# A two-layer hybrid decoder trunk: where the second half of a per-layer input product stands in the order of work

## The chip, the cores and the metric

The kernel runs on one core of one Trainium2 chip. The metric is the device time of one execution in microseconds (us); less is better. Everything is one program: two layers, one after the other, with all weights read from HBM once.

## The reference, cut to what matters

Each of the two layers takes the residual stream h (512 tokens, 1024 features) through three steps:

```
h = h + W_out [ sparse attention heads || mLSTM heads ](RMSNorm(h) @ W_in)
h = h + relu(RMSNorm(h) @ W1)^2 @ W2               # the MLP, 1024 -> 4096 -> 1024
h = h + sigmoid(RMSNorm(h) @ Wg + bg) * (p[i] @ Wp)  # the gated per-layer input, p is 512 x 256
```

The change touches the second and the third step only. p[i] @ Wp, the per-layer input product, does not depend on h at all, so it can be computed at any time before the gate needs it.

## The kernel before, in words

Everything is kept transposed: features on the 128 partitions, the 512 tokens along the free axis. h lies in SBUF as eight tiles of 128x512 (`const` in the trace). Products in float32 are made of three matmuls on a split of each operand into a rounded part hi and a remainder lo: hi*hi, hi*lo, lo*hi (`mm3`).

**Weights.** A weight tile of 128x1024 (512 KB) is loaded by SP into one of 3 buffers `raw`. ScalarE (ACT) writes hi, a rounded copy, into one of 4 buffers `hi`; lo goes into one of 4 buffers `lo`. There are two ways to make lo (`weight`, L521). Most tiles are `adder` tiles: ACT writes -raw rounded, and a DMA issued by GpSimd (POOL) adds. The others subtract hi from raw on VectorE (DVE), or, where `pool` is set, on DVE or POOL as the planner finds it better.

**The MLP** (`mlp`, L1204). Four blocks of the first product (`ff1`) come first. Then 7 shares follow. In share c, two calls of `pair` make four further blocks of the first product, by a scheme with seven products of 12 matmuls with 256 columns each (A12*B21, A11*B11, S1*T1, S2*T2, S3*T3, S4*B22, A22*T4). `pair` gives way (yields) four times, and after each time one output block of the second product of share c (`ff2`) is put in: 12 matmuls with 512 columns, then a DVE add into h. Two output blocks share one weight tile. An eighth share of eight output blocks has no `pair` beside it. The products T1 to T4 use sums of h's tiles, the `forms`, which DVE and ACT make at the MLP's start beside the normal operands (`prep`).

**The per-layer input** (`inputs`, L1180) has two halves, i = 0 and i = 1. Each loads p's two tiles (`s<-pt`, 256 KB each) and one weight tile W_PLE, makes their hi and lo (the label `pw`), and then runs 24 matmuls with 512 columns into four PSUM banks, which ACT copies out (the label `filler`). Half 0 is put into the program ahead of the MLP, half 1 inside the last share, behind its first output block: the buffers and loads of half 1 wait (`nc.hold`) for that block's last operation.

**The gate** (`ple`, L1277) needs the new h, normalised by token, and the four blocks of each half.

**The order.** A planner (`Plan.schedule`, L248) simulates the engines and writes one fixed order for each of the five queues. An operation's rank is the longest way from it to the end, by the planner's own costs, plus 1000 times its label's entry in `URGENT`, and less 1e7 for each later stage; the stages are mix, MLP and gate of layer 0, then of layer 1. A matmul with the label `filler` (-990) is taken only where no other matmul of that stage is ready. `pw` has +145, so these operations go ahead of the MLP's own. Matmuls that carry `nc.chain` keep their program order among themselves: the MLP and the gate are one such chain, `"mlp"`. The filler matmuls are outside it. The planner assumes that a DMA on SP lands 2.2 us after its transfer time, and a DMA from POOL 5.5 us after its issue. At run time each engine works through its queue strictly in this order, and waits on the first instruction that isn't ready. All instructions are issued from one line (L390), so the trace's rows are told apart by tile names and shapes.

Of the kernel before, what the change touches and what calls it, by code (L numbers as in the profile page):

```python
# [33 lines left out]
NFF = 8  # L34
# [9 lines left out]
W_CQ, W_UP, W_QK, W_V, W_O, W_OUT, W_FF1, W_FF2, W_PLE, W_GATE, NW = 0, 2, 4, 12, 16, 20, 28, 60, 92, 94, 102  # L44
# [3 lines left out]

STEP, AHEAD = 5, 8

URGENT = {"start": 325, "squares": 285, "squares0": 90, "setup": -135, "prep": 120, "forms": 120, "norm": 180, "cq": 80, "keys": 55,
          "index": 30, "queries": 45, "gates": 75, "values": 30, "conv": -25, "pw": 145, "filler": -990,
          "attention": -20, "mlstm": 20, "out0": -115, "out1": -145}

# [72 lines left out]
class Plan:  # L127
# [120 lines left out]
    def schedule(self):  # L248
# [9 lines left out]
        for op in ops:  # L258
            op.rank += 1000.0 * (URGENT.get(op.label, 0) + op.bias) - 1e7 * op.stage
        free = {k: list(range(n)) for k, n in self.rooms.items()}  # L260
# [141 lines left out]
class Trunk:  # L402
# [777 lines left out]
    def inputs(self, l, i):  # L1180

        nc = self.nc
        nc.label = "pw"
        raws = [self.slot([128, S]) for _ in range(2)]
        for k in range(2):
            nc.sync.dma_start(raws[k], self.ap["pt"][l, k])
        w = self.wtile(l, W_PLE + i, pool=True)
        pts = []
        for k in range(2):
            hi, lo = self.slot([128, S], F32R), self.slot([128, S], F32R)  # L1190
            nc.scalar.activation(hi, raws[k], AF.Copy)
            nc.vector.tensor_tensor(lo, raws[k], hi.bitcast(F32), op=ALU.subtract)
            pts.append((hi, lo))
        nc.label = "filler"
        for n in range(4):
            ps = self.psum("proj")
            for k in range(2):
                c = slice(k * 512 + n * 128, k * 512 + n * 128 + 128)
                self.mm3(ps, (w[0][:, c], w[1][:, c]), pts[k], k == 0, k == 1)
            o = self.slot([128, S])  # L1200
            nc.scalar.activation(o, ps, AF.Copy, scale=0.5)
            self.pw.setdefault(l, []).append(o)

    def mlp(self, l):  # L1204
        nc = self.nc
        nc.stage = 3 * l + 1
        nc.label = "mlp"
        forms = []
        xs, acc = self.prep(l, C_MLP, forms)
        H = S // 2  # L1210
        lower, upper = slice(0, H), slice(H, S)
        nc.hold = nc.ops[self.mark]
        self.inputs(l, 0)
        nc.hold, nc.label = None, "mlp"
        nc.chain = "mlp"
        fs, state = {}, {}

        def square(i, v):
            hi, lo = self.slot([128, S], F32R), self.slot([128, S], F32R)
            nc.scalar.activation(hi, v, AF.Square)  # L1220
            nc.scalar.activation(v, v, AF.Square)
            nc.vector.tensor_tensor(lo, v, hi.bitcast(F32), op=ALU.subtract)
            fs[i] = (hi, lo)

        def relu(out, u, c=slice(0, S)):
            nc.vector.scalar_tensor_tensor(out, u, 0.0, state["r"][:, c], op0=ALU.max, op1=ALU.mult)

        def ff1(i, n=1, between=None):
            return self.blocks([self.wtile(l, W_FF1 + i + j, adder=True) for j in range(n)], xs, between=between)

        def root():
            state["t"] = self.token_r(acc, D)

        def take(i):
            def act(u0, u1, x):
                relu(u0, u0)
                relu(u1[:, lower], x[:, 0:H], lower)
                relu(u1[:, upper], u1[:, upper], upper)
                square(i, u0)
                square(i + 1, u1)  # L1240
            return act

        def ff2(c):

            for n in range(KD):
                if n % 2 == 0:
                    w = self.wtile(l, W_FF2 + 4 * c + n // 2, adder=True)
                ps = self.psum("proj")
                for k in range(4):
                    o = slice((n % 2) * 512 + k * 128, (n % 2) * 512 + k * 128 + 128)  # L1250
                    self.mm3(ps, (w[0][:, o], w[1][:, o]), fs[4 * c + k], k == 0, k == 3)
                nc.vector.tensor_tensor(self.h[n], self.h[n], ps, op=ALU.add)
                yield n


        pss = ff1(0, 2, root)
        pss += ff1(2)
        state["r"] = self.spread(state["t"])
        pss += ff1(3)
        for i, ps in enumerate(pss):  # L1260
            v = self.slot([128, S], tag="s.v")
            relu(v, ps)
            square(i, v)
        ops = self.operands(xs, forms)
        for c in range(NFF - 1):
            parts = ff2(c)
            for i in (4 * c + 4, 4 * c + 6):
                for _ in self.pair(l, W_FF1 + i, ops, take(i)):
                    next(parts)
        for n in ff2(NFF - 1):  # L1270
            if n == 0:
                nc.hold, nc.chain = nc.ops[-1], None
                self.inputs(l, 1)
                nc.hold, nc.chain, nc.label = None, "mlp", "mlp"
        nc.chain = None

    def ple(self, l):  # L1277
# [138 lines left out]
```

## Time and profile before

| | us |
|---|---|
| median of 3 runs | 1361.09 (1359.71 to 1362.44) |
| the profiled execution | 1356.89 |
| its span (first to last instruction) | 1355.2 |
| TensorE (PE) busy in the span | 1312.2 (97%) |
| VectorE (DVE) busy | 933.1 (69%) |
| ScalarE (ACT) busy | 789.1 (58%) |
| granted TensorE clock, mean | 0.993 |

The trace is of the profiled execution alone. Its 1356.89 us are its span and 1.7 us around it; the median of the separate runs is 4.20 us, or 0.31%, above it. A busy share of PE counts modelled ends of pipelined matmuls, so gaps and the pitch between matmuls say more than the share.

### The profile page before, as it was taken

The page shows a single profiled execution, that of the slowest core. Times are in us where ns is not written, and L with a number is a line of the kernel's source. Part 1 is how long each engine was busy: PE and PEld are TensorE (multiplying, and loading weights), DVE is VectorE, ACT ScalarE, POOL GpSimd, SP SyncE. Part 2 cuts the span into 40 slices and gives each one's busy share as a digit, 9 for nine tenths or more (in the row PEclk, how much of TensorE's full clock was granted, in tenths as well). Part 3 has the DMA queues.
Part 4 walks back from the last instruction along what each step waited for, and adds up shares of the span by engine and source line. Part 5 has one row for each costly group of instructions (what it writes and reads, how often), then busy time and mean ns, then how long its engine had stood idle before and what let it go on. Part 6 is the DMA issues. An engine that isn't in the chain of part 4 may idle for free. (4 is left out here: it accounts for less than half of the span.)

```text
span 1355.2 us, 20154 instructions
## 1 busy us (share of the span) xinstructions
PE 1312.2 (97%) x7376; PEld 1125.9 (83%) x7376; DVE 933.1 (69%) x2049; ACT 789.1 (58%) x1477; POOL 204.5 (15%) x240
## 2 busy tenths in 40 slices
PE   7999999999999999998999999999999999999988
PEld 6877898878888998986887778987798989988877
DVE  7899896576565666644859998848656566665535
ACT  4986684674544545545548947837554554545632
POOL 4132100320100100013112211004010000000210
PEclk9999999999999999999999999999999999999989
DMA  5546801655656555575235576125655655545741
GB/s 191 134 116 170 194 25 44 159 140 156 155 144 161 141 146 140 142 197 144 78 104 125 131 170 166 30 63 140 173 151 145 156 141 156 140 137 140 191 125 63
DMA packets 53092, 183.73 MB, mean 136 GB/s; under 512 B 6272, under 2 KB 6784, under 8 KB 52992
## 3 DMA queue, kind: packets, MB, share of 16 engines
q1 hardware_dynamic: 34848, 116.37, 26.5%
q0 software_dynamic: 18144, 66.07, 26.2%
q8 instruction: 58, 0.95, 0.3%
q14 instruction: 42, 0.34, 0.1%
HBM read 114.25 MB, written 2.10 MB: 86 GB/s over the span
## 5 line engine op out<-in xcount | busy, mean ns | idle before, releaser
L390 PE MATMUL ps_proj<-s,hi 128*128 128x512 f32 (+1 forms) x3184 | 848.7, 356 | 8.0 <-DVE s L390 6.8
L390 PEld LDWEIGHTS ps_proj<-s,hi 128*128 128x128 f32 x3184 | 558.7, 189 | 99.4 <-DVE s L390 9.9
L390 PE MATMUL ps_proj<-s,lo 128*128 128x512 f32 (+1 forms) x1592 | 561.2, 355 | 11.5 <-DVE lo L390 11.5
L390 ACT ACTIVATE hi<-raw 128x1024 fp32r<-128x1024 f32 (+1 forms) x212 | 221.9, 1049 | 253.1 <-PE ps_proj L390 170.9
L390 PEld LDWEIGHTS ps_proj<-s,lo 128*128 128x128 f32 x1592 | 300.3, 189 | 57.1 <-DVE lo L390 13.2
L390 POOL DMA_DIRECT2D lo<-raw x126 | 108.9, 864 | 932.1 <-ACT lo L390 839.7
L390 DVE TENSOR_TENSOR const<-const,ps_proj 128x512 f32<-128x512 f32 x160 | 109.4, 686 | 162.9 <-PE ps_proj L390 162.7
L390 DVE TENSOR_TENSOR lo<-raw,hi 128x1024 fp32r<-128x1024 f32 (+1 forms) x86 | 105.3, 1225 | 115.6 <-ACT hi L390 67.9
L390 ACT ACTIVATE lo<-raw 128x1024 fp32r<-128x1024 f32 x126 | 132.4, 1051 | 9.6 <-PE ps_proj L390 6.5
L390 PE MATMUL ps_proj<-hi,s 128*128 128x512 f32 (+1 forms) x384 | 113.4, 382 | 8.3 <-ACT hi L390 7.6
L390 ACT ACTIVATE s<-s 128x512 fp32r<-128x512 f32 (+2 forms) x154 | 89.3, 619 | 28.9 <-DVE s L390 16.5
L390 DVE TENSOR_TENSOR s<-s,s 128x512 fp32r<-128x512 f32 (+2 forms) x124 | 86.9, 732 | 16.2 <-ACT s L390 15.5
L390 PEld LDWEIGHTS ps_proj<-hi,s 128*128 128x128 f32 x384 | 70.6, 195 | 18.6 <-ACT hi L390 7.6
L390 PE MATMUL ps_sc<-s,s 128*128 128x512 f32 (+3 forms) x288 | 83.4, 376 | 0.6 <-ACT s_idx L390 0.2
L390 POOL TENSOR_TENSOR s<-s,s 128x512 f32<-128x512 f32 x42 | 62.9, 1498 | 91.5 <-ACT s L390 80.8
L390 ACT ACTIVATE s<-ps_proj 128x256 f32<-128x256 f32 (+1 forms) x104 | 41.9, 415 | 54.1 <-PE ps_proj L390 54.1
L390 PE MATMUL ps_proj<-lo,s 128*128 128x512 f32 (+1 forms) x192 | 65.9, 382 | 1.3 <-DVE lo L390 1.3
L390 ACT ACTIVATE s<-raw 128x512 fp32r<-128x512 f32 x28 | 17.6, 628 | 85.0 <-DVE raw L390 85.0
L390 PEld LDWEIGHTS ps_sc<-s,s 128*128 128x128 f32 x288 | 50.6, 190 | 10.6 <-issue 2.2
L390 DVE MATCH_REPLACE8 s<-m,s 128x384 f32<-128x384 f32 (+2 forms) x96 | 51.3, 539 | 0.0
L390 DVE MAX8 m<-s 128x8 f32<-128x384 f32 (+2 forms) x96 | 48.9, 544 | 0.2 <-POOL s L390 0.2
L390 PE MATMUL ps_po<-at,s_et 128*128 128x64 f32 x320 | 48.7, 255 | 0.0
(149 smaller groups left out, 1566.3 us busy)
## 6 DMA issues: line engine op xcount, KB each, us to landing
raw<-ws SPq DMA_DIRECT2D x204, 512.0 KB, 3.6
lo<-raw POOLq DMA_DIRECT2D x126, 512.0 KB, 5.2
raw<-wa SPq DMA_DIRECT2D x8, 336.0 KB, 3.2
const<-xt SPq DMA_DIRECT2D x8, 256.0 KB, 4.6
s<-pt SPq DMA_DIRECT2D x8, 256.0 KB, 7.5
out<-const SPq DMA_DIRECT2D x7, 256.0 KB, 2.0
const<-ct SPq DMA_DIRECT2D x2, 132.0 KB, 3.1
out<-const SPq DMA_DIRECT2D x2, 128.0 KB, 1.7
```

What stands on the lines that cost most here:

```text
L390: ins = getattr(getattr(nc, e), method)(*[value(x) for x in args], **{k: value(x) for k, x in kw.items()}).ins
```

## The change: what it does

1. `inputs` is cut in two. `inputs` now makes the operands only (loads, hi, lo) and returns them; the new `filler` runs the matmuls and the copies. Half 0 calls one behind the other, as before.
2. For half 1, the operands are put into the program ahead of the eighth share, and wait for the last operation of an earlier point (`ahead`): the second `yield` of the last `pair`, that is, ACT's copy of its S2*T2 product. Before, they waited for the first output block of the eighth share.
3. The matmuls of half 1 come behind all output blocks of the eighth share and in the chain `"mlp"`: fixed between the last matmul of the MLP and the first of the gate.
4. For half 1, lo of W_PLE is made on DVE only (`pool=not i`).
5. In each share, the first `yield` of the first `pair` is passed without an output block, so each block of the second product comes one place later, and the eighth one follows behind the second `pair`.
6. `URGENT["forms"]` goes from 120 to 40; `prep` stays at 120.

```
-URGENT = {..., "prep": 120, "forms": 120, "norm": 180, ...
+URGENT = {..., "prep": 120, "forms": 40, "norm": 180, ...

     def inputs(self, l, i):
...
-        w = self.wtile(l, W_PLE + i, pool=True)
+        w = self.wtile(l, W_PLE + i, pool=not i)
         pts = []
         for k in range(2):
             hi, lo = self.slot([128, S], F32R), self.slot([128, S], F32R)
             nc.scalar.activation(hi, raws[k], AF.Copy)
             nc.vector.tensor_tensor(lo, raws[k], hi.bitcast(F32), op=ALU.subtract)
             pts.append((hi, lo))
+        return w, pts
+
+    def filler(self, l, w, pts):
+        nc = self.nc
         nc.label = "filler"
         for n in range(4):
...
-        self.inputs(l, 0)
+        self.filler(l, *self.inputs(l, 0))
...
         for c in range(NFF - 1):
-            parts = ff2(c)
+            parts, n = ff2(c), 0
             for i in (4 * c + 4, 4 * c + 6):
                 for _ in self.pair(l, W_FF1 + i, ops, take(i)):
-                    next(parts)
-        for n in ff2(NFF - 1):
-            if n == 0:
-                nc.hold, nc.chain = nc.ops[-1], None
-                self.inputs(l, 1)
-                nc.hold, nc.chain, nc.label = None, "mlp", "mlp"
+                    if n == 5:
+                        ahead = nc.ops[-1]
+                    if n:
+                        next(parts)
+                    n += 1
+            next(parts)
+        nc.hold = ahead
+        rest = self.inputs(l, 1)
+        nc.hold, nc.label = None, "mlp"
+        for _ in ff2(NFF - 1):
+            pass
+        self.filler(l, *rest)
         nc.chain = None
```

## Rows read from the trace of the kernel before

**Rows 1.** Stretches: us, busy us (instructions) of PE, PEld, DVE, ACT, POOL; clock, DMA share, GB/s

```profile
574.00:595.00 21.00, 21.00 (x131) 18.71 (x131) 11.31 (x19) 10.86 (x16) 2.58 (x3) 1.00 0.62 152
595.00:617.00 22.00, 22.00 (x97) 17.74 (x96) 8.79 (x13) 12.88 (x20) 5.10 (x6) 1.00 0.76 190
```

**Rows 2.** Timeline of PE, both layers' MLP tails: start, duration, operation, [idle before, releaser]

```profile
627.55 0.80 PE L390 MATMUL ps_proj<-s,lo 128*128 128x512 f32 x1 [4.63 <-DVE lo L390]
...
1293.86 1.22 PE L390 MATMUL ps_proj<-s,lo 128*128 128x512 f32 x2 [3.55 <-DVE lo L390]
```

**Rows 3.** The stretches just behind the two stalls of group 2

```profile
627.50:631.00 3.50, 3.45 (x9) 2.73 (x10) 0.66 (x1) 3.50 (x7) 1.53 (x1) 0.54 0.80 274
...
1293.90:1300.00 6.10, 6.10 (x15) 4.80 (x16) 0.57 (x1) 0.67 (x2) 1.51 (x1) 0.52 0.46 173
```

**Rows 4.** Timeline of DVE in the tail of layer 0

```profile
599.35 0.75 DVE L390 SCALAR_TENSOR_TENSOR s<-const,const,s 128x512 fp32r<-128x512 f32 x1 [0.79 <-ACT s L390]
...
616.51 4.28 DVE L390 SCALAR_TENSOR_TENSOR s<-const,const,s 128x512 fp32r<-128x512 f32 x2 [1.53 <-ACT s L390]
...
625.69 0.67 DVE L390 TENSOR_TENSOR const<-const,ps_proj 128x512 f32<-128x512 f32 x1
626.29 1.21 DVE L390 TENSOR_TENSOR lo<-raw,hi 128x1024 fp32r<-128x1024 f32 x1
```

**Rows 5.** Timeline of ACT, then SP, in the tail of layer 0

```profile
611.15 0.63 ACT L390 ACTIVATE s<-s 128x512 fp32r<-128x512 f32 x1 [7.58 <-DMA s<-pt]
...
603.18 0.91 SPq L390 DMA_DIRECT2D s<-pt  x2
```

**Rows 6.** Timeline of PE, stalls inside the two layers' MLPs

```profile
275.33 0.50 PE L390 MATMUL ps_proj<-s,hi 128*128 128x512 f32 x1 [0.92 <-DVE s L390]
...
277.46 0.50 PE L390 MATMUL ps_proj<-s,hi 128*128 128x512 f32 x1 [1.17 <-DVE s L390]
...
303.24 0.50 PE L390 MATMUL ps_proj<-s,hi 128*128 128x512 f32 x1 [1.02 <-DVE s L390]
...
1219.88 0.39 PE L390 MATMUL ps_proj<-s,lo 128*128 128x256 f32 x1 [0.91 <-DVE lo L390]
1243.21 0.39 PE L390 MATMUL ps_proj<-s,lo 128*128 128x256 f32 x1 [2.00 <-DVE lo L390]
```

**Rows 7.** Timeline of DVE just before the stalls at 275 and 277

```profile
272.48 2.80 DVE L390 TENSOR_TENSOR s<-s,s 128x256 f32<-128x256 f32 x4
...
275.53 0.67 DVE L390 TENSOR_TENSOR const<-const,ps_proj 128x512 f32<-128x512 f32 x1
```

**Rows 8.** First and last pair: PE's last A11*B11 matmul, DVE's add of it

```profile
299.53 0.28 PE L390 MATMUL ps_proj<-vx,lo 128*128 128x256 f32 x1
...
301.97 0.42 DVE L390 TENSOR_TENSOR s<-s,ps_proj 128x256 f32<-128x256 f32 x1 [1.24 <-ACT s L390]
...
1245.79 0.28 PE L390 MATMUL ps_proj<-vx,lo 128*128 128x256 f32 x1
...
1246.87 0.41 DVE L390 TENSOR_TENSOR s<-s,ps_proj 128x256 f32<-128x256 f32 x1
```

**Rows 9.** One adder tile through ACT and POOL, ACT's next wait, PEld's wait

```profile
585.48 1.04 ACT L390 ACTIVATE lo<-raw 128x1024 fp32r<-128x1024 f32 x1
...
591.65 0.63 ACT L390 ACTIVATE s<-s 128x512 fp32r<-128x512 f32 x1 [5.12 <-DVE s L390]
...
586.82 0.86 POOL L390 DMA_DIRECT2D lo<-raw  x1 [5.32 <-ACT lo L390]
...
586.35 0.19 PEld L390 LDWEIGHTS ps_proj<-s,lo 128*128 128x128 f32 x1 [0.18 <-DMA lo<-raw]
```

**Rows 10.** DMA issues: tiles, queue, count, KB each, median us to landing

```profile
raw<-ws SPq DMA_DIRECT2D x204, 512.0 KB, 3.6
lo<-raw POOLq DMA_DIRECT2D x126, 512.0 KB, 5.2
...
s<-pt SPq DMA_DIRECT2D x8, 256.0 KB, 7.5
```

More of the change, by code (lines that the diff above doesn't have):

```diff
@@ L49 @@
 STEP, AHEAD = 5, 8
-URGENT = {"start": 325, "squares": 285, "squares0": 90, "setup": -135, "prep": 120, "forms": 120, "norm": 180, "cq": 80, "keys": 55,
+URGENT = {"start": 325, "squares": 285, "squares0": 90, "setup": -135, "prep": 120, "forms": 40, "norm": 180, "cq": 80, "keys": 55,
           "index": 30, "queries": 45, "gates": 75, "values": 30, "conv": -25, "pw": 145, "filler": -990,
```

## The prediction

> **What bounds the kernel now.** I read the stretches first, then the list of PE's stalls, and for each stall the queue of the engine that ended it. In the steady MLP the matmuls leave no gap: 21 and 22 us busy out of 21 and 22, at a granted clock of 1.00 [rows 1]. From 97 matmuls with 512 columns in 22 us I take 0.23 us for one. There nothing is to be won by moving work between the other engines; only PE's stalls count. The reader should look for two groups of them.
>
> The large ones stand behind the MLP, one in each layer: PE waits 4.63 us and 3.55 us for a lo that DVE makes [rows 2]. Afterwards the clock is at the lower of its two levels for a while: 0.54 of full speed over 3.50 us in layer 0, 0.52 over 6.10 us in layer 1 [rows 3]. That costs (1 - 0.54) x 3.50 = 1.6 us and (1 - 0.52) x 6.10 = 2.9 us more. Why is that lo late? In that place only W_PLE of half 1 is a tile of 128x1024 whose lo DVE makes; the gate's first tiles go through POOL. DVE reaches it at 626.29, straight behind the last add into h at 625.69 [rows 4], though PE had been waiting since 627.55 - 4.63 = 622.92. DVE is behind because two of `prep`'s operations, which take 0.75 us each elsewhere, take 4.28 us together at 616.51 [rows 4], and because the whole tail began late: ACT, with p's hi at the head of its queue, stood still 7.58 us until 611.15, as SP had issued p's loads only at 603.18 [rows 5]. So half 1 is both late itself and holds up the gate's operands.
>
> The small ones are at the MLP's start (0.92, 1.17 and 1.02 us in layer 0, and the same three in layer 1), and 0.91 and 2.00 us late in layer 1 only [rows 6].
>
> **The change part by part.** No work is added or removed: the same loads, copies and matmuls run, and DVE made W_PLE's lo for half 1 before, too. All is a matter of order.
>
> *Half 1's operands ahead.* They now wait for ACT's copy of S2*T2 in the last pair. One block (12 x 0.23 = 2.8 us) is already passed over there, and from that copy to the end of the MLP come 12 more output blocks and three small products, some 37 us. Loads of 7.5 us, two hi, two lo and W_PLE's own hi and lo fit in many times. PE then goes from the last output block into the 24 matmuls without a wait: the stalls of 4.63 + 3.55 us and the 1.6 + 2.9 us of low clock go: -12.7 us. What is late next? The gate's first matmuls. Between the MLP and the gate stand half 0's and half 1's matmuls, up to 48 x 0.23 = 11 us as before, and ACT's 7.58 us of standing still in this place are gone too, so `prep` is earlier. I count nothing against the 12.7; the bounds are in a rival.
>
> *The wait moves to the last pair.* ACT will stand at p's hi there: the planner reckons some 3 us from issue to landing, the trace shows 7.5 us [rows 10], so ACT waits about 4.5 us, and DVE, with p's lo, with it. Behind it in ACT's queue stand the next weight tile and the squares for the last share. Before, ACT had a gap of 5.12 us just there, waiting for DVE until 591.65 [rows 9]. So I take 0; if the cover were gone it would be up to 4.5 us a layer.
>
> *A buffer fewer.* W_PLE of half 1 now holds one of the 4 `hi` and one of the 4 `lo` buffers from the last pair to the end of the MLP, and half 0's W_PLE holds another, because its matmuls run only when nothing else can. Two remain for the last share's four adder tiles. Such a tile takes ACT 2 x 1.04, POOL 0.86 [rows 9] and 5.2 us to land [rows 10], about 8.1 us, and then serves 24 matmuls, 5.5 us. Three buffers turn over every 13.6/3 = 4.5 us, less than 5.5, and the trace shows that this is just in time: one matmul waited 0.18 us for such a lo [rows 9]. Two turn over every 6.8 us. The tile that gets its buffer only when A22*T4 is done is needed two output blocks later (5.5 us), so 2.6 to 2.8 us are missing, and as much again two tiles on: 5.6 us a layer at most. But half 0's 24 matmuls (5.5 us) are there to fill just such gaps, and the planner puts them where it foresees one. Between 0 and 5.6 I take 1.5 a layer, nearer to the filled case: +3.0 us.
>
> *Forms at 40.* The stalls at 275.33 and 277.46 wait for `prep`'s lo on DVE [rows 6], and just before them DVE runs forms (halves of 256 columns, 2.80 us for four) [rows 7]. With `prep` above `forms` these go: up to 0.92 + 1.17 us in layer 0 and the same two in layer 1, 4.2 us. But DVE has the same work to do, and the late adds into h (275.53) hold up `prep` as well. Between 0 and -4.2 I take half: -2.1 us.
>
> *Output blocks one place back.* At the first pair, the block whose matmul waited 1.02 us for the squares (303.24) [rows 6] comes 2.8 us later: this stall goes. But S2*T2 now follows A11*B11 after S1*T1 alone (12 matmuls of half the width, 1.4 us), and it writes the bank that DVE's add must have read. That add ended at 302.39, 2.6 us after A11*B11's last matmul [rows 8], so 1.2 us of waiting appear. 0 in sum, between -2.1 and +2.4 over both layers. In the 26 pairs behind the two first ones the same add never ended later than in the last, at 1247.28, 1.2 us after [rows 8]: no wait. In layer 1 the stall of 0.91 us stands at the first pair of a share, which now begins 2.8 us later: -0.9. The one of 2.00 us stands at a second pair, where nothing shifts: it stays.
>
> *A rule weighed.* The last pair's stretch keeps the DMA engines busy 0.62 of the time at 152 GB/s [rows 1]; the 1.0 MB that moves there would need 0.62/152 x 1.0 MB = 4.3 us of full use, and 0.38 x 21 = 8 us are free. The Trainium skill, "DMA: Bandwidth & Descriptors", section "Issuing engines are not separate DMA queues", says that transfers started from any engine end on the same 16 DMA engines and interleave. By the row the move costs 0; by the rule the 4.3 us would fall on the tiles, a rival below.
>
> **The sum.** -12.7 + 3.0 - 2.1 + 0 - 0.9 = -12.7 us, made against the profiled execution: 1356.89 - 12.7 = 1344.2 us. The median of the runs shown stands 4.20 us above that execution, so I forecast a median of 1361.09 - 12.7 = 1348.4 us. Its own range is 1343 to 1354. A measurement of this kernel can tell about 0.2%, 2.7 us, from no change.
>
> **The rivals.**
> *The ring runs dry (slower).* W_PLE's place in the ring is the mechanism, in the last share's eight blocks. If the planner doesn't put half 0's matmuls into these gaps, or puts them where the chip doesn't have the gap, 5.6 us open in each layer, and a gap of nearly 3 us can bring the low clock back (1.6 us or more). If the adder's landing is 2 us longer in that crowd than its median, each of two gaps grows by 2: 5.6 + 4 + 2 = 11.6 a layer, +23 us against -15.7: 1368. It decides from about 8 us a layer. For it speaks the wait of 0.18 us; against it the 24 matmuls that may fill. Chance 0.13.
> *The gate waits next.* If half 0's matmuls are used up in the MLP, only 24, 5.5 us, lie before the gate, and its first adder tile or `prep` could be 3 us late in each layer: 1348.4 + 6 = 1354. Against it: the tail gets back the 7.58 us in which ACT stood still. Chance 0.10.
> *Shared DMA engines.* p's and W_PLE's 1.0 MB pass ahead of the last share's tiles, and these, just in time before, come 4.3 us later in each layer (worked out above from the share and rate of that stretch): 1348.4 + 8.6 = 1357. That 8 us of the stretch are free speaks against. Chance 0.08.
> *The change doesn't do what it says.* Half 1's W_PLE loses its place for a buffer to the MLP's tiles, is made in the tail again, and DVE is as late as before. Then only -2.1 - 0.9 remain: 1358. Against: `pw` stands 145 above the MLP. Chance 0.10.
>
> **How the numbers follow.** The forecast keeps 0.59. The low end, 1342, is all of the forms' 4.2 and none of the ring's 3.0, and some luck at the first pair. The high end, 1360, takes in all cases but the dry ring and part of the unchanged one. Faster by over 0.2%: 0.59 + 0.10 + 0.08 = 0.77; within 0.2%: 0.10; slower: 0.13.
>
> **What would show it.** Right: no wait for DVE's lo behind the MLP in either layer, clock 1.00 through the gate, p's loads in the last pair, ACT's long wait there. The ring: new PE waits for a lo that a DMA adds, in the last share. Forms: no stalls at about 275 and 941. I would be wrong if PE's stall turned up, at the same size, at the gate's first matmuls: then DVE's lateness was the cause, not the place of half 1.

## The result: slower by 1.7%, and the profile after

The changed kernel takes 1384.36 us (median of 4 runs, 1382.05 to 1385.82), the kernel before, in the same series, 1361.76 us (1359.71 to 1362.47). The ratio is 1.0167, with a 95% interval of 1.0148 to 1.0185: 22.6 us slower. Forecast were 1348.4 us and a range up to 1360.

The span of the profiled execution grew from 1355.2 to 1383.0 us. To see where, I take the start of the first A11*B11 matmul (`ps_proj<-vx,hi`) of each pair from the timeline of PE. There are 14 pairs in a layer, so 13 steps; all times in us:

| kernel | first pair, layer 0 | 13 steps, layer 0 | last pair to first pair of layer 1 | 13 steps, layer 1 | last pair to the end | span |
|---|---|---|---|---|---|---|
| before | 298.2 | 276.5 | 389.7 | 280.1 | 110.7 | 1355.2 |
| after | 306.3 | 286.5 | 393.1 | 294.5 | 102.5 | 1383.0 |

With the output blocks one place back the same work is divided otherwise. Before, a step without a gap takes 21.05 us, 13 of them 273.7. After, steps of 18.3 and 23.85 alternate, and 13 without a gap make 271.2 us (a run below shows just that); the 2.5 us that are missing come behind the last pair. With that put right, the change lost 8.1 us before the first pair, 12.5 in the steps of layer 0, 0.9 in the middle part, 16.9 in the steps of layer 1, and won 10.6 at the end: 27.8 us in all. Of the 8.1, 1.5 stand from the first microseconds of this execution on (the first spread of a norm at 30.2 instead of 28.7) and come from no part of the change: two executions of one program below, `e2_half1` and `e4_half1_forms`, start the first pair 1.8 us apart (298.1 and 300.0).

In layer 1 the border between loop and end has moved, too. The planner now puts half 0's 24 matmuls (24 x 0.23 = 5.5 us) into the eleventh step of the loop; before, they stood behind the last pair. ACT's four copies of their results show it; before, these came at 1300 us and later (timeline of ACT, changed kernel):

```profile
1218.56 2.04 ACT L390 ACTIVATE s<-ps_proj 128x512 f32<-128x512 f32 x4
```

So 5.5 of the 16.9 are work that was moved there from the end: the loop of layer 1 lost 11.4, and the end won 5.1.

So the two tail stalls went as forecast, and the loop over the shares lost. These are stretches of the kernel before: the loop in layer 0 and layer 1 (us, then busy us and instructions of PE, PEld, DVE, ACT, POOL; clock, DMA share, GB/s):

```profile
300.00:570.00 270.00, 267.82 (x1676) 240.27 (x1675) 164.92 (x252) 135.74 (x191) 21.51 (x26) 1.00 0.57 149
980.00:1240.00 260.00, 259.10 (x1623) 232.74 (x1622) 158.29 (x242) 129.01 (x181) 19.91 (x24) 1.00 0.55 145
```

And these of the changed kernel: the same two, and the tail of layer 0's MLP:

```profile
300.00:570.00 270.00, 261.67 (x1600) 233.15 (x1600) 154.79 (x240) 130.34 (x185) 20.64 (x24) 0.98 0.54 140
980.00:1240.00 260.00, 250.10 (x1536) 222.69 (x1535) 148.71 (x228) 128.20 (x182) 22.23 (x24) 0.99 0.54 136
617.00:639.00 22.00, 22.00 (x95) 17.88 (x96) 10.74 (x14) 14.49 (x22) 7.44 (x6) 1.00 0.74 188
```

In the tail, where [rows 2, 3] had a stall of 4.63 us and a clock of 0.54, PE is busy without a gap at full clock. In the loop, where PE missed 2.2 of 270 and 0.9 of 260 us, it now misses 8.3 and 9.9, and the mean clock falls to 0.98 and 0.99. The list of PE's waits in the changed kernel (us in total, times, longest) names what is new:

```profile
PE ps_proj L390 <- ACT s L390: 15.8, 11, 3.5
PE ps_proj L390 <- DVE s L390: 11.1, 13, 1.9
...
PE ps_tr L390 <- DVE s L390: 7.1, 4, 3.0
PE ps_proj L390 <- DVE lo L390: 5.1, 6, 1.4
```

Before, the first was 3.5 us in 5 times, the third was not there, and the last was 12.8, with the two tail stalls in it. The two other engines wait, too (changed kernel, list of waits of DVE and of ACT):

```profile
DVE at L390 <- DMA raw<-ws: 83.3, 28, 5.6
...
ACT s L390 <- DVE raw L390: 144.7, 21, 9.4
```

`at` is the first sum of a pair, A21 + A22, which needs the pair's second weight tile. Before, DVE waited for it 8 times, 21.3 us; now in each of the 28 pairs, 83.3 us. That is the thread to follow.

**One round of the changed loop.** The planner's order of the loads on SP, by the tile's number in the list of weights (32 to 59 are the pairs' tiles, two to a pair; 60 and up are output tiles), in the third share:

```
before:  ... 40 41 69 70 42 43 71 72 44 ...
after:   ... 40 68 41 69 42 70 43 71 44 ...
```

Call the pair's tiles r1 and r2. Before, r2 follows r1; after, an output tile stands between them. Timeline of SP in the changed kernel:

```profile
333.42 0.38 SPq L390 DMA_DIRECT2D raw<-ws  x1
...
355.55 0.80 SPq L390 DMA_DIRECT2D raw<-ws  x2
...
364.87 0.33 SPq L390 DMA_DIRECT2D raw<-ws  x1
...
377.20 0.80 SPq L390 DMA_DIRECT2D raw<-ws  x2
...
377.62 0.38 SPq L390 DMA_DIRECT2D raw<-ws  x1
...
488.43 0.38 SPq L390 DMA_DIRECT2D raw<-ws  x1
```

The loads of r2 are those at 333.42, 377.62 and 488.43, and the second of the two at 355.55; always the output tile's load goes out 0.42 us ahead of it. And the engines in the same round (timelines of DVE, ACT, POOL and PE: start, duration, operation, idle time before it and what ended that):

```profile
360.35 0.69 DVE L390 TENSOR_TENSOR at<-raw 128x512 f32<-128x512 f32 x1 [4.00 <-DMA raw<-ws]
...
364.15 0.68 DVE L390 TENSOR_TENSOR s<-raw,s 128x512 fp32r<-128x512 f32 x1
...
372.15 1.22 DVE L390 TENSOR_TENSOR lo<-raw,hi 128x1024 fp32r<-128x1024 f32 x1
...
362.95 0.63 ACT L390 ACTIVATE s<-raw 128x512 fp32r<-128x512 f32 x1 [8.53 <-DVE raw L390]
...
369.63 1.05 ACT L390 ACTIVATE lo<-raw 128x1024 fp32r<-128x1024 f32 x1
...
377.52 1.06 ACT L390 ACTIVATE hi<-raw 128x1024 fp32r<-128x1024 f32 x1 [4.18 <-DMA raw<-ws]
378.49 0.36 ACT L390 ACTIVATE s<-ps_proj 128x256 f32<-128x256 f32 x1
...
370.97 0.86 POOL L390 DMA_DIRECT2D lo<-raw  x1 [5.28 <-ACT lo L390]
...
378.90 1.76 PE L390 MATMUL ps_proj<-s,s 128*128 128x256 f32 x12 [1.77 <-ACT s L390]
380.46 1.06 PE L390 MATMUL ps_proj<-s,hi 128*128 128x512 f32 x2
```

Read as a ring: r2 is there at 360.35 and DVE makes the sums; S3's lo, done at 364.83, frees r1's place. Into that place goes an output tile (load at 364.87). It lands, ACT writes its lo until 370.68, POOL starts the accumulating DMA, and when that has landed the place is free: the next output tile's load goes out at 377.20, and r2's behind it at 377.62. r2's own place had been free since 373.37, when DVE had split A22 out of it (372.15 + 1.22); it stood 4.25 us in SP's queue behind another tile's wait. From one r2 to the next, seven rounds take (488.43 - 333.42) / 7 = 22.14 us each, in layer 1 22.40. TensorE's own round is 21.05. What was ahead at the start is used up, and then PE waits: ACT stands 4.18 us before the next r1, which had its place from an accumulating DMA, too, and behind that stands its copy of S2*T2 (378.49), which S3*T3 needs (1.77 us at 378.90). The matmuls behind come at half the pace (1.06 us for two instead of 0.63). Thirteen rounds that are 1.09 us too long make 14 us; 12.5 were lost in layer 0. (These seven rounds are the regular ones. Over all thirteen, from r2's load at 288.88 to that at 582.92, a round is 22.62 us, 20.4 us too long in all; 7.5 of these are r2's lead on its pair, which shrinks from 17.4 to 9.9 us.)

Before, r2's load stood ahead of the output tile's, went out at 351.64, 0.03 us after DVE had freed its place, and a round took 21.05 us.

### The profile page after: what moved, and what is told of

The parts are those of the page before. It is cut to its first block, busy times and chain, and to the rows that moved or that the text cites. A ratio compares the mean times of both kernels' runs of the same rounds, so it can differ in the third digit from the quotient of the medians.

```text
span 1383.0 us, 20108 instructions
## 1 busy us (share of the span) xinstructions
PE 1322.4 (96%) x7376; PEld 1130.2 (82%) x7376; DVE 922.1 (67%) x2048; ACT 791.1 (57%) x1477; POOL 207.6 (15%) x241
## 5 line engine op out<-in xcount | busy, mean ns | idle before, releaser
L390 DVE TENSOR_TENSOR at<-raw 128x512 f32<-128x512 f32 x28 | 19.4, 693 | 83.3 <-DMA raw<-ws 83.3
L390 PE MATMUL ps_proj<-s,s 128*128 128x256 f32 x336 | 47.2, 292 | 14.6 <-ACT s L390 14.6
L390 PEld LDWEIGHTS ps_proj<-s,s 128*128 128x128 f32 x336 | 44.7, 196 | 19.9 <-ACT s L390 18.2
L390 DVE TENSOR_TENSOR s<-s,ps_proj 128x256 f32<-128x256 f32 x84 | 35.0, 417 | 32.6 <-PE ps_proj L390 32.6
```

Of the source, the lines that this page charges most:

```text
L390: ins = getattr(getattr(nc, e), method)(*[value(x) for x in args], **{k: value(x) for k, x in kw.items()}).ins
```

## The experiments

Theory A: the output blocks' new place costs the time, through the order of SP's loads. Theory B, from the prediction's slower rival: W_PLE's place in the ring of split tiles. Theory C: the forms' urgency. Ratios are to the kernel before in the same series.

### One part at a time

The output blocks alone (`e1_back`), on the kernel before:

```
-            parts = ff2(c)
+            parts, n = ff2(c), 0
...
-                    next(parts)
+                    if n:
+                        next(parts)
+                    n += 1
+            next(parts)
```

> The kernel before with one part of the change alone: the output blocks of the second product stand one place back in every share. Theory A (this part alone costs the time: SP now loads an output block's tile between the two tiles of a pair, the second tile lands later, the preparation on DVE and ACT stands behind it and TensorE waits in the steady MLP): the changed kernel lost 22.6 us and its two stalls and slow stretches at the ends of the MLPs, priced at 12.7 us, are gone, so this part alone is slower by 30 to 36 us, about 1392 to 1397 us, with the second product's first column steps alternating near 18 and 24 us and with S3*T3 stalls in the shares. Theory B (per-layer weight W_PLE in the ring of the split weights costs it): same as before, 1361 us. Theory C (the forms' new urgency costs it): same as before.

Measured: 1392.04 us, ratio 1.0245 (1.0221 to 1.0269).

The per-layer part alone (`e2_half1`): parts 1 to 4 of the change, the output blocks in their old places, forms at 120. Against the changed kernel:

```
-"prep": 120, "forms": 40,
+"prep": 120, "forms": 120,
...
-                    if n:
-                        next(parts)
+                    next(parts)
                     n += 1
-            next(parts)
```

> The kernel before with the per-layer input's part alone: its second half has the fixed place, its operands are made two shares ahead, its weight takes the ring; the output blocks stand where they stood and the forms keep 120. Theory A: the 12.7 us at the ends of the MLPs come back with nothing lost elsewhere, 1347 to 1352 us. Theory B: slower than before by about what the changed kernel lost, 1375 to 1390 us, with stalls on the ring in the last pairs. Theory C: as theory A.

Measured: 1347.71 us, 0.9922 (0.9898 to 0.9946).

The forms alone (`e3_forms`), `"forms": 120` to `"forms": 40`.

> The kernel before with the forms' urgency at 40 alone. Theories A and B: 1359 to 1362 us, no difference that can be told, since the two stalls before the first forms are in the changed kernel as they were. Theory C (with forms later in the queue, norm and forms come later and the whole MLP with them): slower by 15 us or more.

Measured: 1358.74 us, 1.0003 (0.9987 to 1.0020). The setting changes nothing: with 40 as with 120 the planner writes the same instructions in the same order on all five queues, so this is the kernel before, run again.

All but the output blocks (`e4_half1_forms`): the same edit, with the forms left at 40.

> The changed kernel with the output blocks put back in their old places, all else kept. Theory A: as the run with the per-layer part alone, 1347 to 1352 us. Theory B: slower than before, 1375 to 1390 us. Theory C: slower than before, and slower than the run with the per-layer part alone.

Measured: 1350.29 us, 0.9934 (0.9915 to 0.9953). For the same reason this is the program of `e2_half1`, run again; 2.6 us between two medians of one program is the measure for differences of this size.

The loss is the output blocks' alone, +33.7 us, and the per-layer part wins 10.6 us (8.1 in the second run); together +23.1 to +25.6, where the change as a whole gave +22.6. B is out, and so is C, whose edit has no effect. How the place costs the time is not told yet.

### Order of loads, or the place itself

A bias on the pair's two loads changes the order on SP and none of the work:

```
+        nc.bias = 4
         nc.sync.dma_start(r1, self.ap["ws"][l, i])
         nc.sync.dma_start(r2, self.ap["ws"][l, i + 1])
+        nc.bias = 0
```

With the blocks one place back (`e5_back_order`) it brings r1 and r2 together again. In the kernel before (`e7_before_between`) it does the reverse. The rest of the plan is not quite still: between `e1_back` and `e5_back_order` the orders on PE and POOL are the same, but 56 of 242 positions differ on SP, 256 of 1888 on DVE and 126 of 1380 on ACT.

> The kernel before with the output blocks one place back, and with a bias of 4 on the two loads of a pair, by which SP issues them one after the other again (r1, r2, output tile, output tile) as in the kernel before. Theory A1 (the loss is the order of SP's loads: an output tile between the pair's two tiles makes the second late): nearly all of the 33.7 us come back, 1357 to 1366 us. Theory A2 (the loss is the place itself: the add of an output block on DVE, or the bank it keeps, delays what follows, whatever SP's order): stays at 1385 to 1395 us.

Measured: 1366.03 us, 1.0026 (1.0009 to 1.0043): some 30 of the 33.7 us came back.

> The changed kernel, all parts, with the same bias of 4 on the pair's two loads. Theory A1: the per-layer part's gain without the loss, 1346 to 1354 us, faster than before. Theory A2: as the changed kernel, 1380 to 1386 us.

Measured (`e6_after_order`): 1351.12 us, 0.9938 (0.9916 to 0.9961). The changed kernel with two lines more is faster than before.

> The kernel before, output blocks in their old places, with the bias of 4 on the pair's two loads, which there has the opposite effect: SP's order of the weight tiles becomes that of the run with the output blocks one place back (r1, output tile, r2, output tile; 2 of 242 loads differ). Theory A1: the second tile is late here too, slower by 20 to 35 us, 1378 to 1394 us. Theory A2: as before, 1356 to 1362 us.

Measured: 1366.62 us, 1.0047 (1.0030 to 1.0064). Theory A1 missed here: the order alone costs 0.5%, not 2%. The table says where:

| kernel | first pair, layer 0 | 13 steps, layer 0 | last pair to first pair of layer 1 | 13 steps, layer 1 | last pair to the end | span |
|---|---|---|---|---|---|---|
| `e1_back` | 306.3 | 284.5 | 398.9 | 283.3 | 115.4 | 1388.4 |
| `e5_back_order` | 304.8 | 271.4 | 400.8 | 272.1 | 114.2 | 1363.3 |
| `e7_before_between` | 304.5 | 275.6 | 396.5 | 279.9 | 110.5 | 1367.0 |

In `e7_before_between` the steps are as before, and the time goes before the first pair of either layer (298.2 to 304.5, and 389.7 to 396.5). So there are two losses: a late first pair, which the order alone brings (`e7_before_between`) and the place alone, too (`e5_back_order`, 304.8), and a slow loop, for which order and place must come together. The stretch of the loop in layer 0, `e5_back_order`, then `e7_before_between`:

```profile
300.00:570.00 270.00, 270.00 (x1692) 242.82 (x1691) 162.90 (x250) 138.76 (x193) 23.94 (x26) 1.00 0.57 150
```

```profile
300.00:570.00 270.00, 269.09 (x1680) 241.37 (x1680) 162.61 (x248) 136.45 (x192) 23.98 (x26) 1.00 0.55 145
```

Why is the loop whole in `e7_before_between`? There, too, a pair's load goes out 0.42 us behind an output tile's, each time the second of two (r2's in the first and the third row, the next r1's in the second):

```profile
353.59 0.80 SPq L390 DMA_DIRECT2D raw<-ws  x2
...
364.74 0.80 SPq L390 DMA_DIRECT2D raw<-ws  x2
...
374.38 0.80 SPq L390 DMA_DIRECT2D raw<-ws  x2
```

But by the planner's assignment of places the output tiles follow each other in one place there (their loads are the first at 353.59, 364.74 and 374.38), and neither waits for S3. This round, counted over the seven as above from the traces' SP rows, is 21.46 us in layer 0: longer than 21.05 as well, but by 0.4, and what is ahead at the start covers most of it. With the blocks one place back the output tile takes r1's place, and DVE's sums come into the round: 22.14 us. In `e5_back_order` it is 21.03.

### Shortening the round

Four places for arriving tiles (`e8_back_ring4`), and 58 s slots for 60, with the blocks one place back and their order as it falls:

```
-ROOMS = {"s": 60, "raw": 3, ...
+ROOMS = {"s": 58, "raw": 4, ...
```

> The output blocks one place back, SP's order left as that makes it, but four places for arriving weight tiles in place of three (and 58 s slots in place of 60, so that it fits). Theory A1 with the ring of three as what holds the second tile's load back: the load goes out as soon as its turn comes, 1358 to 1375 us. If the order alone hurts (two loads at once share the engines, both land late) and the ring has no part in it: 1385 to 1395 us.

Measured: 1359.06 us, 0.9989 (0.9970 to 1.0008): the loss is gone. r2's rounds take 21.05 us, though r2 is still loaded behind an output tile.

The blocks one place back and three places, but no accumulating DMA for the output tiles (`e11_back_noadd`):

```
-                    w = self.wtile(l, W_FF2 + 4 * c + n // 2, adder=True)
+                    w = self.wtile(l, W_FF2 + 4 * c + n // 2)
...
+        nc.bias = -6
         nc.sync.dma_start(r2, self.ap["ws"][l, i + 1])
+        nc.bias = 0
```

> Output blocks one place back, three places, SP's loads between one another as that makes them (a bias of -6 on the second load keeps that order), but the low half of an output tile is subtracted on DVE in place of the copy on ACT and the accumulating DMA, so that the tile's place comes free with the subtraction. If the round r2, S3, output tile, accumulating DMA, output tile, r2 is what takes 22.2 us in place of TensorE's 21.05, the five and more us of the DMA drop out of it and the steps go back to 21.05: 1357 to 1370 us (the 56 subtractions of 1.2 us fall on DVE, which has room for them in the mean). If it is the two loads going out together that hurts, whatever frees the place: 1385 us or more.

Measured: 1346.74 us, 0.9910 (0.9889 to 0.9931). Not only is the loss gone: with no part of the per-layer change, it is 0.9% faster than before, below what I expected. Its loop in layer 0 and PE's waits in the whole span:

```profile
300.00:570.00 270.00, 270.00 (x1694) 242.81 (x1693) 196.75 (x279) 115.27 (x168) 0.00 (x0) 1.00 0.32 102
```

```profile
PE ps_proj L390 <- ACT hi L390: 7.9, 2, 7.5
PE ps_tr L390 <- DVE s L390: 7.6, 4, 3.4
PE ps_proj L390 <- DVE s L390: 4.8, 6, 1.2
```

DVE is busy 196.75 of 270 us, more than before (164.92), and PE waits for nothing there; the DMA engines' share is 0.32, against 0.55 in `e1_back`. The two tail stalls are not in the list either, though half 1 was not touched. The edit reaches the last share's tiles as well (64 of the 126 accumulating DMAs are gone, and so is what SP waited for there). First SP's waits in the kernel before from 590 to 604 us (us in total, times, longest), where p's loads go out at 603.18 [rows 5] behind them, then p's loads in this run:

```profile
SPq L390 <- DMA lo<-raw: 14.8, 3, 7.3
```

```profile
595.64 0.86 SPq L390 DMA_DIRECT2D s<-pt  x2
```

In this run SP waits for no such DMA in that stretch, and DVE has W_PLE's lo at 611.79 instead of 627.50. In layer 1 p's loads go out at 1257.92 instead of 1272.02. Read from these traces, the tail stalls, too, hung on how fast the weight tiles' places come free: p's loads stood in SP's queue behind loads that waited for a place.

### Combinations

The per-layer part alone with four places (`e9_half1_ring4`):

> The run with the per-layer part alone (1347.7 us, ratio 0.992 to before), with four places for arriving weight tiles and 58 s slots. If the ring of three also holds the tuned order back a little (in the run with four places and blocks one place back the loss of 33.7 us went, and 2.4 us more), 0.986 to 0.991 of before, 1342 to 1349 us; if the loops are TensorE's own already, the same ratio as with three places, 0.991 to 0.994.

Measured: 1349.67 us, 0.9930 (0.9909 to 0.9952): no gain from the fourth place. Its loop is not quite TensorE's own: r2's seven rounds take 22.03 us in layer 0, against 21.05 with three places. By the planner's assignment r2 there takes a place that an accumulating DMA frees (load at 390.46); DVE's sum waits 6.91 us for it (395.14), and PE 0.93 us for DVE (399.69). Which place a tile takes counts, and not only how many there are.

The changed kernel with the same four places (`e10_after_ring4`):

> The changed kernel, all parts, with four places for arriving weight tiles and 58 s slots. If the loss is the round of the three places, it goes here as in the run with the output blocks alone: 1343 to 1352 us, faster than before by 0.6 to 1.2%. If the per-layer part needs what the fourth place took from the s slots, above 1356 us.

Measured: 1344.34 us, 0.9895 (0.9867 to 0.9922).

The changed kernel with the edit of `e11_back_noadd` (`e12_after_noadd`):

> The changed kernel, all parts, with the output tiles' low half subtracted on DVE and the same bias of -6 on the second load. If the gains add up (the per-layer part 0.8% of before, the subtraction with the blocks one place back 0.9%), 0.981 to 0.985 of before, 1334 to 1340 us; if both get back the same stalls behind the MLP, 0.988 to 0.992, 1343 to 1350 us.

Measured: 1345.89 us, 0.9916 (0.9894 to 0.9938). The gains do not add: with the tail stalls gone already, the per-layer part has none left to take away.

### The late first pair

Open was why the first pair starts 6 us late in each run with three places in which the blocks or the order are moved, `e5_back_order` with its old order included. In the changed kernel DVE and PE show this (timelines):

```profile
289.42 0.15 DVE L390 TENSOR_TENSOR tiny<-tiny,tiny 128x4 f32<-128x4 f32 x1
292.46 0.69 DVE L390 TENSOR_TENSOR at<-raw 128x512 f32<-128x512 f32 x1 [2.89 <-DMA raw<-ws]
293.07 0.15 DVE L390 SCALAR_TENSOR_TENSOR tiny<-tiny,tiny 128x4 f32<-128x4 f32 x1
...
295.26 0.80 PE L390 MATMUL ps_tr<-s,const 128*128 128x512 f32 x1 [2.86 <-DVE s L390]
296.54 0.79 PE L390 MATMUL ps_tr<-s,const 128*128 128x512 f32 x1 [0.48 <-DVE s L390]
297.13 1.05 PE L390 MATMUL ps_proj<-s,hi 128*128 128x512 f32 x2
```

In the norm's chain of twelve tiny operations, behind the tenth, stands the pair's first sum, which waits 2.89 us for r2. The other late runs show the same: in `e5_back_order` and `e7_before_between` the sum stands ahead of the norm's last operations, too, and waits 3.86 and 3.01 us; in the kernel before it comes behind them. PE waits at the norm's spread, 2.86 and 0.48 us, and then runs at half the pace (1.05 us for two matmuls). Two runs hold that one sum back, in the planner, behind the spread's last operation on DVE:

```
             nc.tensor.matmul(ps, self.onesr, d4.flat(), start=i == 0, stop=i == 1)
+        self.spreads = nc.ops[-2]
...
+        nc.hold = self.spreads
         nc.vector.tensor_tensor(r3[:, a], r2[:, a], r2[:, b], op=ALU.add)
+        nc.hold = None
```

> The changed kernel with that one sum held and nothing else: the loop keeps its late second tile. If the sum's place is the cause of the late start, 6 to 13 us faster than the changed kernel, 1370 to 1378 us, still slower than before by 0.8 to 1.3%; if not, 1380 to 1386 us.

Measured (`e14_after_hold`, the changed kernel with that alone): 1371.36 us, 1.0112 (1.0064 to 1.0160). The first pair starts at 298.2 and the middle part is 384.7 us instead of 393.1; the steps keep their loss (287.1 and 296.3).

> The run with all parts and the subtraction on DVE (0.992 of before, first A11*B11 at 304.3 us), with the pair's first sum on DVE held behind the norm's chain. If DVE's place for that sum is what stops TensorE (3.3 us and 0.8 us, and some 2 us of matmuls at half clock, in either layer), both stalls go and the time falls by 8 to 12 us: 0.983 to 0.986 of before, 1335 to 1340 us, and the stretch from 275 to 300 us is at full clock. If it is the order of the loads, 1343 to 1348 us as without.

Measured (`e13_after_noadd_hold`): 1339.51 us, 0.9873 (0.9835 to 0.9911), the lowest ratio of all (its interval overlaps that of `e10_after_ring4`). The stretch of the MLP's start in `e12_after_noadd`, which lacks the hold alone, then in this one, and in this one the sum in its new place and what is left of PE's wait:

```profile
275.00:300.00 25.00, 19.56 (x78) 15.15 (x79) 18.70 (x39) 15.83 (x27) 3.22 (x3) 0.93 0.43 106
```

```profile
275.00:300.00 25.00, 22.36 (x104) 17.79 (x105) 19.74 (x41) 17.65 (x30) 3.22 (x3) 1.00 0.44 106
```

```profile
291.20 1.29 DVE L390 TENSOR_TENSOR s<-const,tiny 128x512 fp32r<-128x512 f32 x2
292.41 0.69 DVE L390 TENSOR_TENSOR at<-raw 128x512 f32<-128x512 f32 x1
...
291.94 1.10 PE L390 MATMUL ps_tr<-s,const 128*128 128x512 f32 x2 [1.26 <-DVE s L390]
```

The clock stays at 1.00 instead of 0.93. A wait of 1.26 us is left, since two splits that wait for ACT (1.19 and 1.71 us) still stand between the tiny operations. The gain, 5.8 us by the two ratios and 6.9 between the profiled spans, is under the expected 8 to 12.

## Why the prediction was wrong

**The step that failed is *Output blocks one place back*: "0 in sum", and "in the 26 pairs behind the two first ones ... no wait".** Measured alone it is +33.7 us. I moved 12 matmuls and asked only whether DVE's add of A11*B11 comes in time for S2*T2. (It does: at the first pair the feared wait of 1.2 us did not come, the add ends 0.53 us behind the last matmul.) But an output block carries its tile with it: SP's load, ACT's two copies, POOL's DMA. The planner ranks these by when the block is due; one block later they fell behind r1 and ahead of r2. The question that was left out is which loads now stand between a pair's two, and whose wait they bring into SP's queue.

**The view that misled is the gapless stretch [rows 1],** of the last pair and the first blocks behind it. From it I took that in the steady loop nothing is to be won, and let that count as nothing to be lost. A round of three places that runs at TensorE's 21.05 us shows no stall, whether it has 0.1 us to spare or 10. [Rows 9, 10] held the terms: an adder tile keeps a place through its load, ACT's copies and the DMA. I used them for the ring of four `hi` and `lo` in the last share, and not for the ring of three `raw` in the other shares.

***Half 1's operands ahead***, -12.7 us: the mechanism was right. Both tail stalls are gone after the change, and the run with this part alone won 10.6 us (7.3 to 13.9 by the interval of its ratio). Its size differs by layer. In the profiled executions the middle part shrinks by only 0.6 us (389.7 to 389.1), where 6.2 were forecast. The part behind the last pair of layer 1 shrinks by 9.3 (110.7 to 101.4), but 4.4 of that are 19 of half 0's matmuls, which here, too, now stand in the eleventh step of the loop: 4.9 are won, where 6.5 were forecast. The loop of layer 1 takes 281.2 us with these 4.4 in it, against 280.1, so 3.3 more come from there: the stalls of 0.91 and 2.00 us [rows 6], of which the prediction let the second stay. In layer 0 the last share pays: these are PE's stalls there with this part alone (timeline of PE, `e2_half1`):

```profile
595.83 0.50 PE L390 MATMUL ps_proj<-s,lo 128*128 128x512 f32 x1 [0.77 <-DMA lo<-raw]
597.34 1.43 PE L390 MATMUL ps_proj<-s,hi 128*128 128x512 f32 x5 [0.31 <-ACT s L390]
600.49 0.50 PE L390 MATMUL ps_proj<-s,hi 128*128 128x512 f32 x1 [1.03 <-DVE s L390]
602.48 0.50 PE L390 MATMUL ps_proj<-s,hi 128*128 128x512 f32 x1 [1.03 <-DVE s L390]
```

That is 3.1 us; and in the stretch from 603 to 607 us, just behind, the granted clock is 0.57, 1.7 us more: 4.8 of the 5.6 us that are missing there.

***A buffer fewer* and *The wait moves to the last pair*,** +3.0 and 0: together with the 12.7 they make -9.7, against -10.6 and -8.1 in the two runs of this program, and -8.7 between the two profiled spans. That this fits is in part luck, since the parts don't. Of the stalls above only the first, 0.77 us, is a wait for an adder tile's lo. The other 2.4 us wait for ACT, and for what DVE makes behind ACT, and ACT stands still for p's two tiles (timeline of ACT, `e2_half1`):

```profile
589.73 0.63 ACT L390 ACTIVATE s<-s 128x512 fp32r<-128x512 f32 x1 [3.12 <-DMA s<-pt]
596.13 1.16 ACT L390 ACTIVATE s<-s 128x512 fp32r<-128x512 f32 x2 [5.77 <-DMA s<-pt]
```

These are 8.9 us, where I reckoned with 4.5 and took the cover for enough: the term put at 0 cost at least 2.4 us in layer 0. The rival of the ring running dry, as I had placed it, did not come. What ran slow was the other ring.

***Forms at 40*,** -2.1: nothing, and not by chance. The planner writes the same order with 40 as with 120, so the rank of `forms` against `prep` decides nothing there, and comparing the two orders would have shown it. The stalls at 275 and 277 [rows 6] are there after the change, at 276.77 with 0.91 us and at 278.92 with 1.17.

***A rule weighed*.** By the row the move of 1.0 MB costs nothing, and no wait of the size of the rival's 4.3 us for a weight tile came with it: with the per-layer part alone PE waits 0.77 us and 0.82 us for an adder tile's lo. On the pair's tiles there is a small term: from r2's issue to DVE's use it is 4.37 us when an output tile goes out 0.42 us ahead (377.62 to 381.99 in the changed kernel), and 3.47 us in `e5_back_order` when r2 goes first (353.02 to 356.49). The Trainium skill, "DMA: Bandwidth & Descriptors", section "Issuing engines are not separate DMA queues", says that all transfers interleave on the same engines. The trace agrees with it here by these 0.9 us. They are one term of the long round; in `e7_before_between`, where r2 takes 4.41 us as well (354.01 to 358.42), the steps stay as before.

**The chances.** Slower had 0.13, all of it from another mechanism. None of the rivals was a new order of the loads in the loop, though one rank decides the order on all five queues.

What stays open: that the places' assignment is what lengthens the round of `e1_back` against `e7_before_between` is read from the two traces; the runs that shorten the round agree with it, but none changed the assignment alone, and the bias that restores the order on SP also moves operations on DVE and ACT.

## What to carry to other kernels

When a list scheduler places a step by its due time, moving the step moves its loads: before costing the move, write down the order of loads it brings on each queue, and for each ring of buffers the closed round (land, use, free, next load, land). A stretch in which TensorE has no gap shows that this round is no longer than TensorE's (or that tiles loaded ahead still cover it), not how much shorter it is, so it can turn into the bound by one microsecond and cost that in every turn. A load that is ready can stand behind one that is not: put loads that are needed together next to each other (here that took back 30 of 33.7 us), and give the slow way of freeing a place (here an accumulating DMA) to a ring with a place to spare.

## What the runs showed of the hardware that was not expected

The list of DMA issues of the changed kernel (tiles, queue, count, KB each, median us from issue to landing), against 3.6, 5.2 and 7.5 us in [rows 10]:

```profile
raw<-ws SPq DMA_DIRECT2D x204, 512.0 KB, 4.2
lo<-raw POOLq DMA_DIRECT2D x126, 512.0 KB, 5.6
s<-pt SPq DMA_DIRECT2D x8, 256.0 KB, 7.3
```

SP's weight tiles land 0.6 us later in the median; against 3.6 in the kernel before it is 4.1 in `e7_before_between`, too, where the loads' order alone is changed. The accumulating DMAs land 0.4 us later, and why is not shown: in `e7_before_between`, with the loads between one another as well, it is 4.9. And 1.2 us of DVE for a tile's lo was cheaper here than ACT's second copy (1.05 us), POOL's issue (0.86 us) and the accumulating DMA: with the subtraction on DVE the busy share of the DMA engines in the loop fell from 0.55 to 0.32, and from ACT's hi to the next load into the tile's place it took 1.3 us (409.81 to 411.09) instead of 7.5 (369.72 to 377.20 in the changed kernel).
